# A hybrid decoder block on one core: the values' weights of one stage prepared earlier and partly on VectorE, and the last output weights prepared early

## The chip, the cores and the metric

The kernel runs on one core of a Trainium2 chip. The metric is device time in microseconds (us): the median of several executions. Before the change it is 588.81 us over 3 runs (588.73 to 589.13). The core has five engines that this document names as the profile does: PE (TensorE, the matrix engine; PEld is its weight load), DVE (VectorE), ACT (ScalarE), POOL (GpSimd) and SP (SyncE, which here issues all DMAs). Each engine serves its own queue of instructions in order and waits on semaphores for the others.

## The reference

One layer of a decoder block with two attention branches over 528 tokens (16 learned meta tokens and 512 real ones), width 1024:

```python
u = rmsnorm(h, pre_norm_g)
(cq, ckv, k_pe_raw, z_mla, fq, fk, fv, f_logit, z_fox, gate_a, gate_b) = split(u @ w_in)
# branch 1, MLA: 16 heads, low-rank queries, keys and values, rotary part of 32
q  = rmsnorm(cq)  @ w_uq
kv = rmsnorm(ckv) @ w_ukv
y_mla = (attention(q_m, k_m, v_mla) * silu(z_mla)) @ w_br_mla
# branch 2, FoX: 16 heads of 64, with a cumulative forget bias on the scores
cum = cumsum(log_sigmoid(f_logit + fox_forget_b))
y_fox = (attention(fq, fk, fv, bias=cum) * silu(z_fox)) @ w_br_fox
mixed = (sigmoid(gate_a) * y_mla + sigmoid(gate_b) * y_fox) @ w_out
out = h + rmsnorm(mixed, post_norm_g)          # meta tokens dropped
```

All inputs and outputs are float32. Attention is causal.

## The kernel before, in words

**Precision by halves.** Matmul operands are split into an upper half (`wh`, a rounded copy made on ACT) and a lower half (`wl`, the value less its upper half), and each product is three matmuls: upper by upper, upper by lower, lower by upper. `wsplit` (line 126) does this for a block of weights that was loaded as `wraw`: a cast 128x1024 on ACT (line 131), then a subtract on the engine that `low[0]` names, through `split_lo` (line 104). `low[0]` is POOL in the attention part, and DVE in the parts after it (line 1027). The tiles `wraw`, `wh` and `wl` come from a pool of three buffers each (line 84), so a cast waits for the buffer of an earlier block to be free.

**Units and fills.** A projection is a `unit` (line 176): a list of small steps of three matmuls each. Its `prep` splits the weights; its first step calls `prep` if nothing has called it before, and then issues the loads of the next three units. Steps of units are mixed between the attention's own work: `fills` has one list for each of 16 stages. A stage is one branch and one pair of heads, FoX and MLA in turn; stage 0 is FoX, stage 1 (`si == 1`) the MLA stage of the first pair. The fill of stage 1 is, in order: one transpose of values, the 8 steps of the FoX queries of the next pair (fq), the first 8 steps of its keys (fk), the 16 steps of its values (v, from step 17 on), and the last 8 steps of the keys.

**A stage** (lines 984 to 1016) takes scores on PE, evicts them with a mask or bias on DVE, takes exponentials on ACT (line 821), and normalises in two groups, `n0` (three query blocks) and `n1` (one): sums and reciprocals on DVE, then for each block and head a scaled upper half on ACT (line 850) and a lower half on DVE (line 851). POOL handles the leading 16 columns. The results are transposed by DMA for the value product (`ov`), which is written behind the scores of the next stage.

**What sets the order.** In the attention and after it, PE's matmuls run in the order in which the code writes them. The queues of the other engines are put in order when the program is built: each time an engine is free in the builder's own picture of the run, it takes the ready instruction with the smallest number, which is the place where it was written. `high_priority(offset=n)` writes instructions as if they stood n places earlier. `issue_after(x)` adds an edge: not ahead of x in x's queue. `keep_in_program_order` adds an edge to the instruction written just before on the same engine. In stage 1 the list `behind` holds the last exponential of the first three query blocks, so that the weight casts of this stage stand behind it on ACT (line 993). The order on the chip is then fixed.

In stage 1 before the change, v's weights are split when the fill comes to step 17, so in the code after both normalisations. SP issues v's load ahead of four small stores of rotary queries (`qpe_dram`) and of a transpose of values.

**The output projection** (from line 1262) is one level of Strassen's scheme: seven block products into accumulators X, Y, Z of two row blocks each, with sums of activations (`sh`, `sl`, `a1`, `a2`) and of weights (`tb`) made beforehand. `plain` and `summed` split the weights of half a product through the three-buffer pool. The last product adds the weight sum `tb[3]` times `a2` into X, which still holds the sum that rows 2 and 3 need in their other half; DVE must have read X before the last product writes on. Its weights `w4` are split in two pieces, the second behind the read of X. Then each row block is normalised: squares on ACT, `first_sum`, `scaled_g`, and `finish_t` (root, reciprocal, scale and residual) with two stores per block. Row blocks 0 and 1 are finished while the last products run, 2 and 3 at the end.

Of the kernel before, what the change touches and what calls it, by code (L numbers as in the profile page):

```python
# [17 lines left out]
ALU = mybir.AluOpType  # L18
# [4 lines left out]
D = 1024  # L23
# [5 lines left out]
EPS = 1e-6  # L29
# [26 lines left out]
def block_kernel(ctx: ExitStack, tc: tile.TileContext, x, meta_tokens, pre_norm_g, w_in, fox_forget_b,  # L56
                 mla_q_norm_g, mla_kv_norm_g, w_uq, w_ukv, w_br_mla, w_br_fox, w_out, post_norm_g,
                 rope_tok, rope_pe, out):
    nc = tc.nc
# [43 lines left out]
    def split_lo(eng, lo, src, hi):  # L103
        return eng.tensor_tensor(out=lo, in0=src, in1=f32(hi), op=ALU.subtract)  # L104
# [19 lines left out]
    low = [nc.gpsimd]  # L124
# [98 lines left out]
    def run(steps):  # L223
        for _, fn in steps:
            fn()
# [33 lines left out]
    with ExitStack() as ph:  # L259
# [33 lines left out]
        for c in range(4):  # L293
            r = pa.tile([128, 2, NSM], F32, tag="wsr", name=f"wsr{c}", bufs=4)
# [146 lines left out]
        pin = tc.keep_in_program_order  # L441
# [100 lines left out]
    with ExitStack() as att:  # L542
# [384 lines left out]
        for si, (br, pr) in enumerate(stages):  # L927
            last = si + 1 == len(stages)
            if not last:
                q, k, v = feed(*stages[si + 1])  # L930
            if br == 1:

                za, zb = z_unit(1, pr), z_unit(0, pr)
                fill = (vts[br, pr] if pr else begun) + za + q + zb[:3] + k + zb[3:5] + v + zb[5:]
            elif not last:

                fill = vts[br, pr] + q + k[:KD] + v + k[KD:]
            else:
                g = gate_unit()
                fill = vts[br, pr] + g + gate_unit() + gate_unit()  # L940
# [22 lines left out]
        for si, (br, pr) in enumerate(stages):  # L963
            last = si + 1 == len(stages)
            sc, n0, n1, va = attention(br, pr)

            fill = fills[si]
            sc()
            for fn in late:
                fn()  # L970
            if si == 0:

                run(fill[:5])
                run(vts[1, 0] + pe_rest)
                n0()
                bias(1)
                low[0] = nc.vector
                for ahead_ in [fn.prep for _, fn in fill[5:] if hasattr(fn, "prep")][:2]:
                    with tc.issue_after(whole[0]):
                        ahead_()  # L980
                low[0] = nc.gpsimd
                n1()
                run(fill[5:])
            else:
                if si == 1:
                    stores(2, 4)
                run(fill[:3])
                if si == 3:
                    stores(4, 8)
                run(fill[3:5])  # L990
                if si == 1:

                    behind[:] = exps[:1]
                if si == 2:
                    behind.clear()
                n0()
                if pr and not (br or last):
                    bias(pr + 1)
                run(fill[5:11])
                if br:  # L1000

                    behind[:] = [halved[("k", 1, pr), 1]]
                run(fill[11:12])
                if br:
                    behind.clear()
                n1()
                if not (br or last):
                    masked_bias()
                if 6 <= si < 8:

# [17 lines left out]
    with ExitStack() as mg:  # L1028
# [8 lines left out]
        tb = [m1.tile([128, HK, 512], F32, tag=f"tb{n}", name=f"tb{n}") for n in range(4)]  # L1037
        a1 = [m1.tile([128, HK, 256], F32R, tag=n, name=n) for n in ("a1h", "a1l")]
        a2 = [m1.tile([128, HK, S], F32R, tag=n, name=n) for n in ("a2h", "a2l")]
        mx = gT[0]  # L1040
        sh, sl = ([t.rearrange("p k s -> p (k s)")[:, 1024 * j : 1024 * j + 1024].rearrange("p (k s) -> p k s", k=HK)
                   for j in range(4)] for t in uT0)
# [164 lines left out]
        yo, xr = (o1.tile([128, 4, D], F32, tag=n, name=n) for n in ("yo", "xr"))  # L1207
        gp = o1.tile([128, D], F32, tag="gp", name="gp")
        ss = pad[:, 16:32].rearrange("p (t n) -> p t n", t=4)
# [10 lines left out]
        def summed(n, c):  # L1220
            uid[0] += 1
            raw = tb[n][:, 2 * c : 2 * c + 2].rearrange("p k f -> p (k f)")
            return by_k(wsplit((uid[0], raw, [(0, 1024)], 1024))[0], 2)

        def block(ps, a, t0, w, c, r, first, last, cs=slice(0, 512)):

            q = 0
            for kk in range(2):
                k = 2 * c + kk
                ts = slice(t0 + 128 * r, t0 + 128 * r + 128)  # L1230
                for x, b in ((a[0], w[0]), (a[1], w[0]), (a[0], w[1])):
                    mm(ps[r][:, cs], x[:, k, ts], b(kk)[:, cs], start=(first and c == 0 and q == 0), stop=(last and c == 1 and q == 5),
                       skip_group_check=True)
                    q += 1
# [7 lines left out]
        def squares_of(src, t, n, w=512):  # L1242
            nc.scalar.activation(jk[:, :w], src, AF.Square, accum_out=ss[:, t, n : n + 1])

        def first_sum(t, n):
            nc.vector.tensor_scalar(out=ss[:, t, 2:3], in0=ss[:, t, n : n + 1], scalar1=1.0 / D, scalar2=4.0 * EPS,
                                    op0=ALU.mult, op1=ALU.add)

        def scaled_g(t, sl, src=None):
            nc.vector.tensor_tensor(out=yo[:, t, sl], in0=yo[:, t, sl] if src is None else src, in1=gp[:, sl], op=ALU.mult)  # L1250

        def finish_t(t, n, order):
            nc.scalar.activation(ss[:, t, 3:4], ss[:, t, n : n + 1], AF.Sqrt, bias=ss[:, t, 2:3], scale=1.0 / D)
            nc.vector.reciprocal(ss[:, t, 3:4], ss[:, t, 3:4])
            for sl_ in order:
                nc.vector.scalar_tensor_tensor(out=yo[:, t, sl_], in0=yo[:, t, sl_], scalar=ss[:, t, 3:4],
                                               in1=xr[:, t, sl_], op0=ALU.mult, op1=ALU.add)
                nc.sync.dma_start(out2[128 * t : 128 * t + 128, sl_], yo[:, t, sl_])

        X, Z = ([op5.tile([128, 512], F32, tag="po", name=f"{n}{r}") for r in range(2)] for n in "xz")  # L1260
# [17 lines left out]
        product(Z, s_[3], 0, lambda c: plain(1, 1, c), False, True)  # L1278
        w7 = [summed(1, c) for c in range(2)]
        for r in range(2):  # L1280
            nc.vector.tensor_tensor(out=yo[:, r, N1], in0=Z[r], in1=yo[:, r, N1], op=ALU.add)
            squares_of(yo[:, r, N1], r, 1)
        w4 = [summed(3, 0)]
        for c in range(2):
            for r in range(2):
                block(X, s_[2], 0, w7[c], c, r, False, False)
                if c:
                    read = nc.vector.tensor_tensor(out=yo[:, 2 + r, N1], in0=X[r], in1=yo[:, 2 + r, N1], op=ALU.add)
                    if not r:
                        with tc.issue_after(read.ins):  # L1290
                            w4.append(summed(3, 1))
                    squares_of(yo[:, 2 + r, N1], 2 + r, 1)
                    first_sum(2 + r, 1)
        for r in range(2):
            scaled_g(r, N1)
            finish_t(r, 1, (N0, N1))
        for r in range(2):
            scaled_g(2 + r, N1)
        for r in range(2):
# [48 lines left out]
```

## Time and profile before

| | before |
|---|---|
| median of 3 runs | 588.81 us |
| the profiled execution | 589.07 us, span 587.1 us |
| granted PE clock, mean | 0.997 |
| PE busy | 577.8 us, 98% of the span |
| DVE busy | 419.4 us, 71% |
| ACT busy | 357.1 us, 61% |
| POOL busy | 199.0 us, 34% |
| DMA | 97.46 MB, mean 166 GB/s |

How to read the lines in the next part: a line of a timeline is the start in us from the begin of the span, the duration, the engine, the line of code, the operation, output and inputs by the program's names, the shape, and the count; in brackets the idle time of the engine before it and what ended it. In the list of waits the three numbers are us in total, times, and the longest. In the chain of waits a line is a start, a length, and what the chain was in. A table of stretches has, for each stretch, the busy time of PE, PEld, DVE, ACT and POOL with the number of instructions, then the granted PE clock, the share of the DMA engines and GB/s. A line of a DMA list ends with us from issue to landing. PE is busy nearly throughout, so what counts is where it stops.

### The profile page before, as it was taken

How to read it: one execution, taken by the hardware profiler on the slowest of the kernel's cores; microseconds unless marked ns; L12 is line 12 of the kernel's file. 1: busy time of each engine (PE TensorE's matmuls, PEld its weight loads, DVE VectorE, ACT ScalarE, POOL GpSimd, SP SyncE). 2: the span in 40 equal slices, each digit the busy share in tenths (PEclk: the TensorE clock that was granted, in tenths of full speed). 3: DMA queues.
4: the chain of work that ended last, by engine and by line, in shares of the span. 5: the costliest groups of instructions: out<-in, count | busy, mean ns of one | idle time of the engine just before them, and what ended most of it. 6: DMA issues, size and time to landing. Idle time of an engine off the chain costs nothing.

```text
span 587.1 us, 11116 instructions
## 1 busy us (share of the span) xinstructions
PE 577.8 (98%) x3841; PEld 497.7 (85%) x3841; DVE 419.4 (71%) x1155; ACT 357.1 (61%) x816; POOL 199.0 (34%) x271
## 2 busy tenths in 40 slices
PE   8999999999999999999999999999999999999996
PEld 6889888889889889888898898878998998888884
DVE  5854878884785775767758748896657876468957
ACT  7846774783783785767748747944343462443663
POOL 4317646464467472554544634510000000000000
PEclk9999999999999999999999999999999999999998
DMA  8535598999978999988987976877622544233603
GB/s 292 122 86 162 123 179 194 236 180 285 169 169 157 228 189 210 221 173 206 180 174 181 220 153 147 183 170 264 202 74 70 144 108 139 77 109 107 216 0 143
DMA packets 219999, 97.46 MB, mean 166 GB/s; under 512 B 131456, under 2 KB 209672, under 8 KB 219944
## 3 DMA queue, kind: packets, MB, share of 16 engines
q1 hardware_dynamic: 219944, 96.77, 69.5%
q8 instruction: 30, 0.49, 0.3%
q14 instruction: 25, 0.20, 0.1%
HBM read 62.36 MB, written 3.97 MB: 113 GB/s over the span
## 4 chain that ended last, share of the span: by engine, by line
PE 83%; POOL 1%; issue 0%; DVE 0%; DVEq 0%; ACT 0%; POOLq 0%
PE z L98 17%; PE pg L98 14%; PE v L98 8%; PE x L98 8%; PE py L98 7%; PE st L98 7%; PE fk L98 6%; PE fq L98 6%; PE ov L98 5%; PE y L98 2%; PE mq L98 2%; PE mk L98 1%; POOL wl L104 1%; PE ppe L98 0%; POOL mt L837 0%
## 5 line engine op out<-in xcount | busy, mean ns | idle before, releaser
L104 POOL TENSOR_TENSOR wl<-wraw,wh 128x1024 fp32r<-128x1024 f32 (+2 forms) x62 | 120.2, 1947 | 112.6 <-ACT wh L131 79.6
L131 ACT CAST wh<-wraw 128x1024 fp32r<-128x1024 f32 (+1 forms) x72 | 74.6, 1040 | 58.2 <-PE py L98 16.8
L821 ACT ACTIVATE sf<-sf,nb 128x272 f32<-128x272 f32 (+3 forms) x128 | 72.7, 569 | 11.2 <-DVE nb L786 10.2
L851 DVE SCALAR_TENSOR_TENSOR pn<-sf,ri,pn 128x512 f16<-128x512 f32 (+3 forms) x128 | 73.6, 641 | 2.1 <-ACT pn L850 1.9
L104 DVE TENSOR_TENSOR wl<-wraw,wh 128x512 fp32r<-128x512 f32 (+1 forms) x54 | 51.0, 947 | 28.6 <-ACT wh L1085 20.0
L850 ACT ACTIVATE pn<-sf,ri 128x128 f16<-128x128 f32 (+3 forms) x128 | 59.7, 548 | 0.0
L98 PE MATMUL z<-uTh,wh 128*128 128x512 f32 x128 | 50.9, 398 | 0.0
L98 PE MATMUL pg<-uTh,wh 128*128 128x512 f32 x128 | 50.2, 392 | 0.0
L98 PE MATMUL z<-uTl,wh 128*128 128x512 f32 x128 | 50.1, 391 | 0.0
L98 PE MATMUL z<-uTh,wl 128*128 128x512 f32 x128 | 50.0, 390 | 0.0
L98 PE MATMUL pg<-uTl,wh 128*128 128x512 f32 x128 | 49.9, 390 | 0.0
L98 PE MATMUL pg<-uTh,wl 128*128 128x512 f32 x128 | 49.8, 389 | 0.0
L98 PE MATMUL st<-hlk,hlq 64*128 64x272 f32 (+4 forms) x480 | 41.3, 299 | 0.0
L1085 ACT CAST wh<-wraw 128x512 fp32r<-128x512 f32 x28 | 17.3, 619 | 38.6 <-DVE wraw L1094 14.3
L701 DVE TENSOR_REDUCE vsc<-v 128x1 f32<-128x272 f32 (+1 forms) x32 | 13.2, 432 | 36.7 <-PE v L98 36.7
L98 PE MATMUL v<-uTh,wl 128*128 128x256 f32 (+1 forms) x128 | 36.6, 286 | 1.1 <-POOL wl L104 1.1
L98 PE MATMUL fk<-uTl,wh 128*128 128x256 f32 (+1 forms) x128 | 36.4, 285 | 0.0
L98 PEld LDWEIGHTS st<-hlk,hlq 64*128 64x128 f32 x480 | 33.0, 186 | 4.1 <-ACT vh L720 2.8
L98 PE MATMUL fk<-uTh,wh 128*128 128x256 f32 (+1 forms) x128 | 36.4, 285 | 0.0
L98 PE MATMUL v<-uTl,wh 128*128 128x256 f32 (+1 forms) x128 | 36.4, 285 | 0.0
L98 PE MATMUL fk<-uTh,wl 128*128 128x256 f32 (+1 forms) x128 | 36.4, 285 | 0.0
L98 PE MATMUL v<-uTh,wh 128*128 128x256 f32 (+1 forms) x128 | 36.4, 284 | 0.0
(285 smaller groups left out, 1611.5 us busy)
## 6 DMA issues: line engine op xcount, KB each, us to landing
wraw<-in_w_in_dram SPq DMA_DIRECT2D x56, 512.0 KB, 4.9
cbp<-c_dram SPq DMA_DIRECT2D x16, 264.0 KB, 3.9
wraw<-in_w_br_fox_dram SPq DMA_DIRECT2D x8, 512.0 KB, 4.7
tb<-in_w_out_dram SPq DMA_DIRECT2D x8, 512.0 KB, 5.2
wraw<-in_w_br_mla_dram SPq DMA_DIRECT2D x8, 512.0 KB, 4.1
wraw<-in_w_out_dram SPq DMA_DIRECT2D x6, 512.0 KB, 3.8
xr<-in_x_dram SPq DMA_DIRECT2D x4, 512.0 KB
out_dram<-yo SPq DMA_DIRECT2D x8, 256.0 KB, 2.0
```

Of the source, the lines that this page charges most:

```text
L98: nc.tensor.matmul(*a, **k)
L104: return eng.tensor_tensor(out=lo, in0=src, in1=f32(hi), op=ALU.subtract)
L131: nc.scalar.copy(wh[:, :n], raw[:, :n])
L701: nc.vector.tensor_reduce(out=sc[:, i : i + 1], in_=ps, op=ALU.max, axis=AX.X, apply_absolute_value=True)
L821: exps[b // 3] = nc.scalar.activation(sf, sf, AF.Exp, bias=sums["nb"][:, h, b : b + 1], scale=-1.0, accum_out=sums["su"][:, h, b : b + 1]).ins
L850: normed[:] = [nc.scalar.activation(hi, sf, AF.Copy, scale=rib).ins]
L851: nc.vector.scalar_tensor_tensor(out=lo, in0=sf, scalar=rib, in1=hi, op0=ALU.mult, op1=ALU.subtract)
L1085: nc.scalar.copy(to[0], src)
```

## The change

There are two edits.

In stage 1, after six further steps of the fill (which hold the split of fk's weights), the split of v's weights is written there and then, with a priority offset of 60, and its lower half goes to VectorE in place of GpSimd. It stands before the code of `n1`, and by its priority before `n0`. Step 17 later finds the weights split and only issues its matmuls and the next loads.

In the output projection the last product's weights no longer go through the three-buffer pool. A new function, `put_in`, splits both pieces into tiles whose last use lies several products back (`a1` and the first of the `sh`, `sl` pairs), and is written before the last two products. The vector instructions of the epilogue keep the order in which they are written (`pin`), and that order is changed: row blocks 0 and 1 are scaled and block 0 finished before the reads of X for rows 2 and 3, and block 1 is finished between these two reads.

```diff
@@ -997,6 +997,11 @@
                 if pr and not (br or last):
                     bias(pr + 1)
                 run(fill[5:11])
+                if si == 1:
+                    low[0] = nc.vector
+                    with tc.high_priority(offset=60):
+                        fill[17][1].prep()
+                    low[0] = nc.gpsimd
                 if br:
@@ -1222,6 +1227,15 @@
+        def put_in(n, c, to):
+            raw = tb[n][:, 2 * c : 2 * c + 2]
+            hi, lo = (t.rearrange("p k s -> p (k s)").rearrange("p (k f) -> p k f", k=2) for t in to)
+            nc.scalar.copy(hi, raw)
+            split_lo(nc.vector, lo, raw, hi)
+            return (lambda k: hi[:, k]), (lambda k: lo[:, k])
+
+        pin = tc.keep_in_program_order
...
         def first_sum(t, n):
-            nc.vector.tensor_scalar(...)
+            pin(nc.vector.tensor_scalar(...))
...
@@ -1278,22 +1292,22 @@
         w7 = [summed(1, c) for c in range(2)]
         for r in range(2):
-            nc.vector.tensor_tensor(out=yo[:, r, N1], in0=Z[r], in1=yo[:, r, N1], op=ALU.add)
+            pin(nc.vector.tensor_tensor(out=yo[:, r, N1], in0=Z[r], in1=yo[:, r, N1], op=ALU.add))
             squares_of(yo[:, r, N1], r, 1)
-        w4 = [summed(3, 0)]
+        w4 = [put_in(3, c, to) for c, to in enumerate((a1, s_[0]))]
+        for r in range(2):
+            scaled_g(r, N1)
+        finish_t(0, 1, (N0, N1))
         for c in range(2):
             for r in range(2):
                 block(X, s_[2], 0, w7[c], c, r, False, False)
-                if c:
-                    read = nc.vector.tensor_tensor(out=yo[:, 2 + r, N1], in0=X[r], in1=yo[:, 2 + r, N1], op=ALU.add)
-                    if not r:
-                        with tc.issue_after(read.ins):
-                            w4.append(summed(3, 1))
-                    squares_of(yo[:, 2 + r, N1], 2 + r, 1)
-                    first_sum(2 + r, 1)
         for r in range(2):
-            scaled_g(r, N1)
-            finish_t(r, 1, (N0, N1))
+            pin(nc.vector.tensor_tensor(out=yo[:, 2 + r, N1], in0=X[r], in1=yo[:, 2 + r, N1], op=ALU.add))
+            squares_of(yo[:, 2 + r, N1], 2 + r, 1)
+            if not r:
+                finish_t(1, 1, (N0, N1))
+        for r in range(2):
+            first_sum(2 + r, 1)
         for r in range(2):
             scaled_g(2 + r, N1)
```

The vector instructions in `scaled_g` and `finish_t` are pinned in the same way.

More of the change, by code (lines that the diff above doesn't have):

```diff
@@ L1245, in first_sum @@
         def first_sum(t, n):
-            nc.vector.tensor_scalar(out=ss[:, t, 2:3], in0=ss[:, t, n : n + 1], scalar1=1.0 / D, scalar2=4.0 * EPS,
-                                    op0=ALU.mult, op1=ALU.add)
+            pin(nc.vector.tensor_scalar(out=ss[:, t, 2:3], in0=ss[:, t, n : n + 1], scalar1=1.0 / D, scalar2=4.0 * EPS,
+                                        op0=ALU.mult, op1=ALU.add))
         def scaled_g(t, sl, src=None):
-            nc.vector.tensor_tensor(out=yo[:, t, sl], in0=yo[:, t, sl] if src is None else src, in1=gp[:, sl], op=ALU.mult)
+            pin(nc.vector.tensor_tensor(out=yo[:, t, sl], in0=yo[:, t, sl] if src is None else src, in1=gp[:, sl], op=ALU.mult))
         def finish_t(t, n, order):
             nc.scalar.activation(ss[:, t, 3:4], ss[:, t, n : n + 1], AF.Sqrt, bias=ss[:, t, 2:3], scale=1.0 / D)
-            nc.vector.reciprocal(ss[:, t, 3:4], ss[:, t, 3:4])
+            pin(nc.vector.reciprocal(ss[:, t, 3:4], ss[:, t, 3:4]))
             for sl_ in order:
-                nc.vector.scalar_tensor_tensor(out=yo[:, t, sl_], in0=yo[:, t, sl_], scalar=ss[:, t, 3:4],
-                                               in1=xr[:, t, sl_], op0=ALU.mult, op1=ALU.add)
+                pin(nc.vector.scalar_tensor_tensor(out=yo[:, t, sl_], in0=yo[:, t, sl_], scalar=ss[:, t, 3:4],
+                                                   in1=xr[:, t, sl_], op0=ALU.mult, op1=ALU.add))
                 nc.sync.dma_start(out2[128 * t : 128 * t + 128, sl_], yo[:, t, sl_])
```

## The prediction

> **What bounds the kernel now.** I read the page first, then the waits of the matmul engine, then the chain of waits, and only then the timelines around the two places that the change touches.
>
> ```profile
> span 587.1 us, 11116 instructions
> PE 83%; POOL 1%; issue 0%; DVE 0%; DVEq 0%; ACT 0%; POOLq 0%
> ```
>
> ```profile
> PE spun L98 <- DVE KPL L233: 1.5, 1, 1.5
> PE v L98 <- POOL wl L104: 1.1, 1, 1.1
> ```
>
> ```profile
> 91.04 2.52 POOL wl L104
> 93.56 0.04 issue
> 93.61 5.86 PE v L98 x46
> ...
> 575.53 5.75 PE x L98 x24
> ```
>
> PE is the bound. In the list of waits its largest stall outside the start is one of 1.1 us: the matmuls of v wait for a lower half (wl) made on POOL. From 93.61 to 581.29 the chain runs through PE alone. So a microsecond won or lost on PE at 93 us reaches the end in full: nothing later is idle and could absorb it. Behind 581.29 lies a tail of vector work and stores. The first edit aims at the 1.1 us stall, the second at the work around the tail.
>
> The stage around the stall, PE first, then POOL, ScalarE (ACT) and VectorE (DVE):
>
> ```profile
> 89.17 0.29 PE L98 MATMUL fk<-uTh,wh 128*128 128x272 f32 x1
> ...
> 89.42 0.29 PE L98 MATMUL fk<-uTh,wl 128*128 128x272 f32 x1
> ...
> 92.14 0.29 PE L98 MATMUL v<-uTh,wh 128*128 128x272 f32 x1
> 92.26 0.28 PE L98 MATMUL v<-uTl,wh 128*128 128x272 f32 x1
> 93.61 0.39 PE L98 MATMUL v<-uTh,wl 128*128 128x272 f32 x1 [1.06 <-POOL wl L104]
> ```
>
> ```profile
> 86.77 2.41 POOL L104 TENSOR_TENSOR wl<-wraw,wh 128x1024 fp32r<-128x1024 f32 x1
> ...
> 91.00 2.55 POOL L104 TENSOR_TENSOR wl<-wraw,wh 128x1024 fp32r<-128x1024 f32 x1
> ```
>
> ```profile
> 84.42 0.62 ACT L821 ACTIVATE sf<-sf,nb 128x400 f32<-128x400 f32 x1
> ...
> 85.03 1.04 ACT L131 CAST wh<-wraw 128x1024 fp32r<-128x1024 f32 x1
> 85.98 1.01 ACT L850 ACTIVATE pn<-sf,ri 128x512 f16<-128x512 f32 x2
> ```
>
> ```profile
> 89.61 1.04 ACT L131 CAST wh<-wraw 128x1024 fp32r<-128x1024 f32 x1
> ```
>
> Matched by order: the cast at 85.03 and the POOL subtract at 86.77 are fk's weights, ready at 89.18 for their first use at 89.42. The cast at 89.61 and the subtract at 91.00 are v's. Matmuls of this shape follow each other at 0.12 us (two steps from 89.17 to 89.42, one from 92.14 to 92.26), so v's third one was due at 92.38; it starts at 93.61, a loss of 1.23 us.
>
> **Edit 1, the halves of v.** It adds nothing and removes nothing. One ACT cast and one subtract are traced earlier, with a priority 60 instructions further up, and the subtract goes from POOL (2.55) to VectorE (1.22, first row below). No DMA is issued in it: v's load was issued by the unit before.
>
> ```profile
> L104 DVE TENSOR_TENSOR wl<-wraw,wh 128x1024 fp32r<-128x1024 f32 x26 | 31.7, 1222 | 8.5 <-ACT wh L131 8.1
> ```
>
> ```profile
> 86.73 3.00 DVE L851 SCALAR_TENSOR_TENSOR pn<-sf,ri,pn 128x512 f16<-128x512 f32 x1 [0.60 <-ACT pn L850]
> ```
>
> What it can win is the 1.23 us of v. On VectorE 1.22 us come in, and a blockage goes: the product at 86.73 takes 3.00 us while POOL's subtract of 86.77 runs. That is even or better, and beside PE's work.
>
> What it costs hangs on the place of the cast in ACT's queue, which is served in order, and on when v's raw weights are there:
>
> ```profile
> 78.47 0.56 SPq L92 DMA_DIRECT2D wraw<-in_w_in_dram  x1
> ```
>
> ```profile
> wraw<-in_w_in_dram SPq DMA_DIRECT2D x1, 512.0 KB, 10.7
> ```
>
> ```profile
> 86.00:89.00 3.00, 3.00 (x15) 2.49 (x14) 2.40 (x3) 3.00 (x8) 3.00 (x4) 1.00 0.15 43
> ```
>
> The load issued at 78.47 needs 10.7 us to land, so v's raw weights are complete only at about 89.2; from 86 to 89 the DMA moves 43 GB/s at a share of 0.15, with the stores to qpe_dram and a transpose issued behind this load. In the kernel before that is hidden: the cast stands behind all eight products (L850) and starts at 89.61. In the new one it may stand right behind the last exponential (84.42): its only order edge is to that instruction, and its priority lies ahead of fk's cast and of the products. The list order is made when the program is built, with its own picture of when a load lands, and that picture is early:
>
> ```profile
> 105.58 1.05 ACT L131 CAST wh<-wraw 128x1024 fp32r<-128x1024 f32 x1 [2.83 <-DMA wraw<-in_w_in_dram]
> ```
>
> Here ACT already stands 2.83 us before a cast whose load is not in, with exponentials queued behind it. I expect the same at 85.1 us, for longer.
>
> Step by step, if v's cast is first: ACT waits from 85.1 to 89.2, and v's cast runs. The next cast starts 0.95 later (85.03 to 85.98 is that spacing) at 90.15, and fk's upper half is there at 91.2. POOL's subtract follows at 91.25 and takes 2.41, to 93.65, and PE's third fk matmul starts 0.05 after that (as at 93.56 to 93.61, which I take for the hand-over before it too), at 93.7 instead of 89.42: **+4.3 us**. v's lower half is ready at 90.25 + 1.2 = 91.5, long before v starts at 96.4, so the old stall goes: **-1.2 us**. Queued behind the waiting cast are fk's cast, the eight products that fill ACT from 85.98 to 89.61, and the eviction of fq; the products start about 4 us late, and so do the transposes that the next ov needs.
>
> ```profile
> 98.35 3.23 SPq L92 DMA_TRANSPOSE pt<-pn  x1
> ```
>
> ```profile
> 104.45 0.62 PE L98 MATMUL ov<-pt,vp 80*64 80x512 f16 x4
> ```
>
> ```profile
> out_dram<-yo SPq DMA_DIRECT2D x8, 256.0 KB, 2.0
> ```
>
> The last of these is issued until 101.58; with the 2.0 us that the nearest listed small transfer needs to land it is in at about 103.6, 0.9 us ahead of ov. PE's own 3 us of delay move ov to 107.5, so this chain has 3 us more and I cost it at nothing. Without PE's delay it would be the next thing late: ov would be due at 104.45 - 1.2 = 103.2, and 0.4 us or more would come back.
>
> PE then has two pauses, 89.17 to 91.25 and 91.5 to 93.7, with two matmuls between. What the clock does in a pause can be read at the two ends of the run:
>
> ```profile
> 581.30:583.00 1.70, 0.00 (x0) 0.00 (x0) 1.59 (x4) 0.98 (x3) 0.00 (x0) 1.00 0.49 190
> 583.00:584.00 1.00, 0.00 (x0) 0.00 (x0) 1.00 (x2) 0.00 (x0) 0.00 (x0) 0.81 0.52 201
> 584.00:585.00 1.00, 0.00 (x0) 0.00 (x0) 0.24 (x1) 0.00 (x0) 0.00 (x0) 0.50 0.56 221
> ```
>
> ```profile
> 1.45 4.64 PE L98 MATMUL spun<-KPL 128*128 128x512 f32 x10 [1.45 <-DVE KPL L233]
> ```
>
> The granted clock goes from 1.00 to 0.50 within 583 to 584 (mean 0.81, so at about 583.6), 2.3 us after the last matmul. At the start ten matmuls of 512 columns take 4.64 us, 0.46 each, where in the last product they follow at 0.23 (574.90 and 575.13 below). So two pauses of 2.1 and 2.2 us in a stretch of 4.5 probably halve the clock, and getting it back costs 10 x 0.23 = **+2.3 us** (from 0, if it stays, to 2.9, if it takes a quarter longer). I take 2.3, the measured start.
>
> **Edit 2, the last weights.** Two casts (1.05 each) and two subtracts (1.22 each) move from around 570 to 576 into idle time before, into tiles that their last product has left; the DVE order is pinned. No load is added; the stores keep their number.
>
> ```profile
> 574.04 0.75 DVE L1256 SCALAR_TENSOR_TENSOR yo<-yo,pad,xr 128x512 f32<-128x512 f32 x1
> 574.70 0.69 DVE L1288 TENSOR_TENSOR yo<-x,yo 128x512 f32<-128x512 f32 x1
> ```
>
> ```profile
> 574.90 0.39 PE L98 MATMUL x<-wh,uTl 128*128 128x512 f32 x1
> 575.13 0.39 PE L98 MATMUL x<-wl,uTh 128*128 128x512 f32 x1
> 575.53 0.47 PE L98 MATMUL x<-wh,a2h 128*128 128x512 f32 x1
> ```
>
> The last product may overwrite X only when VectorE has read it (574.70 to 575.39); PE starts at 575.53 where 575.36 was due, and its next one 0.31 later instead of 0.23: 0.25 us lost. Without the subtract of the last weights VectorE is done with the first row block about a microsecond sooner and reads X when it is complete: **-0.2 us**. The other read of X now stands behind 1.4 us of finishing work, ends near 577.3, and is needed at 578.1.
>
> ```profile
> 560.09 1.23 DVE L104 TENSOR_TENSOR wl<-wraw,wh 128x1024 fp32r<-128x1024 f32 x1 [1.49 <-ACT wh L131]
> ```
>
> ```profile
> 581.31 0.58 ACT L1243 ACTIVATE jk<-x 128x512 f32<-128x512 f32 x1 [1.68 <-PE x L98]
> ```
>
> Gaps such as the 1.49 us before 560.09 hold a moved subtract; if one collides, a product waits a few tenths (the other end, +0.4). The tail does not shorten: it starts with the squares at 581.31, which wait for PE, and VectorE is free by then in both kernels.
>
> Sum against the profiled execution (589.07 us, span 587.1; 0.26 above the median of 588.81): +4.3 - 1.2 + 2.3 - 0.2 = +5.2, so 594.3 there and **594.0** against the median.
>
> **Rivals.** *The clock stays (591.7).* Neither pause alone is longer than the 2.3 us after which it fell at the end, and two matmuls lie between. Then the 2.3 falls away. For it: the 1.06 us pause at 93.61 left the clock alone; against it, 4.3 of 4.5 us idle. The Trainium skill's page "TensorE: Matmul & The Clock Gate", in Part 1, section "What's actually happening", gives the low clock after at least one idle window of about 3.4 us, free-running. By that rule this rival wins when no window lies in the pauses; the drop 2.3 us after the last matmul says that a window need not be idle throughout.
>
> *fk's cast goes first (587.6, the other side).* If the order puts fk's cast at 85.03 as now and v's next, fk is untouched and v's lower half is ready at 91.5 for 92.38: -1.2 and -0.2, with 0 to 0.4 back at ov because the products wait from 86 to 89.2. That is 587.4 to 587.8. It decides in which order two casts stand behind one exponential. Against it: v's priority is the higher, and its load was issued only 0.6 us after fk's.
>
> *No block (587.4).* If the order takes v's load as landed late, the cast falls among or behind the products: 588.81 - 1.2 - 0.2. For it speaks nothing in the trace; the 2.83 us wait speaks against it.
>
> *Worse.* If fk's cast also falls behind six of the eight products (6/8 of 3.63 us, 2.7), 597.
>
> **How the numbers follow.** Block with the clock halved 0.52, block with the clock kept 0.14, fk first 0.14, no block 0.15, worse or something else 0.05. The prediction is that of the likeliest, 594.0, its own range 592.8 to 595.2 (clock loss 1.7 to 2.9, edit 2 from -0.3 to +0.4). The range over the cases is 587.3 to 595.2. About 0.2%, 1.2 us, is what a measurement of this kernel can tell from no change. Slower: the first two and most of the rest, 0.70. The gains are -1.0 to -1.4 us, some inside that bound: faster 0.21, same 0.09.
>
> **What would show it.** Right: ACT idle for about 4 us behind the last exponential at 85.1, ended by a DMA; the two casts back to back from 89.2; PE waiting on fk's upper and lower halves in place of v's; granted clock at 0.50 for some 4 us from about 93; the products ending later; X read at 574.4 of the old clock with no gap in front of the last product. Wrong: fk's first matmul at 89.17 as before; no idle time of ACT at 85; or a load of v that lands well before 89.

## The result, and the profile after

The changed kernel takes 587.89 us (median) beside 588.88 us before. The ratio is 0.9983 with a 95% interval of 0.9975 to 0.9990: a gain of 0.17%, about 1 us. A second measurement beside other kernels gave 587.89 beside 589.01, a ratio of 0.9981 (0.9973 to 0.9990). The profiled execution took 587.82 us, and its page begins with

```profile
span 586.0 us, 11114 instructions
```

In the list of waits of the matmul engine (what it waited for: total, times, longest) the entry for v is gone, and a new one, for ov, stands in it (one of 0.6 us for psm, near the start of the program, is gone too, but comes back with 0.9 in a second profile of the same kernel):

```profile
PE spun L98 <- DVE KPL L233: 1.4, 1, 1.4
PE ov L98 <- DMA pt<-pn: 0.5, 2, 0.2
PE pt L101 <- DVE uTl L366: 0.3, 1, 0.3
```

The stage around the old stall, in the timeline after the change (start, duration, engine), ScalarE first, then GpSimd, VectorE, PE and the SP queue:

```profile
84.65 0.19 ACT L821 ACTIVATION_READ_ACCUMULATOR sf<-sf,nb 128x1 f32 x1
84.74 1.99 ACT L131 CAST wh<-wraw 128x1024 fp32r<-128x1024 f32 x2
86.63 3.74 ACT L850 ACTIVATE pn<-sf,ri 128x128 f16<-128x128 f32 x8
...
86.47 2.41 POOL L104 TENSOR_TENSOR wl<-wraw,wh 128x1024 fp32r<-128x1024 f32 x1
...
86.76 3.19 DVE L104 TENSOR_TENSOR wl<-wraw,wh 128x1024 fp32r<-128x1024 f32 x1 [0.93 <-ACT wh L131]
89.88 4.05 DVE L851 SCALAR_TENSOR_TENSOR pn<-sf,ri,pn 128x128 f16<-128x128 f32 x8
...
92.23 0.28 PE L98 MATMUL v<-uTl,wh 128*128 128x272 f32 x1
92.36 0.29 PE L98 MATMUL v<-uTh,wl 128*128 128x272 f32 x1
...
90.46 0.42 SPq L92 DMA_DIRECT2D wraw<-in_w_in_dram  x1
91.30 3.98 SPq L92 DMA_TRANSPOSE pt<-pn  x2
```

Two casts run back to back at 84.74, with no wait between the last exponential and them, and the eight products follow. GpSimd's subtract (fk's lower half) starts at 86.47, about where it did before (86.77), and VectorE's (v's) at 86.76, as the second cast ends. So the first of the two casts is fk's and the second is v's. v's lower half is there at 89.95, and its third matmul starts at 92.36, 0.13 behind its neighbour at 92.23: the stall of 1.23 us is gone. On the SP queue a load of raw weights now stands ahead of the four transposes; before, all four stood ahead of it:

```profile
91.07 10.51 SPq L92 DMA_TRANSPOSE pt<-pn  x4
101.67 2.29 SPq L92 DMA_DIRECT2D wraw<-in_w_in_dram  x3
```

What lets it go earlier is v's raw buffer, whose last reader is v's subtract (in a second profile, below, the load is issued at 90.65 and the subtract ends at 90.63). The chain of waits shows where it ends:

```profile
98.61 4.67 DMA pt<-pn
103.28 0.14 issue
103.41 2.04 PE ov L98 x26
```

The last transpose, issued at 98.61, lands at 103.28, and ov waits for it. The second edit shows in the timeline of the last product (X read on VectorE, then PE):

```profile
573.20 0.69 DVE L1305 TENSOR_TENSOR yo<-x,yo 128x512 f32<-128x512 f32 x1 [0.17 <-PE x L98]
...
574.13 0.39 PE L98 MATMUL x<-wl,uTh 128*128 128x512 f32 x1
574.36 0.39 PE L98 MATMUL x<-a1h,a2h 128*128 128x512 f32 x1
```

The read of X starts 1.16 us before the last product (574.36) needs its place and ends 0.47 us before it, and the matmuls go on at 0.23.

A ledger from the starts of PE's matmuls is the best way to compare these profiles, because the first fk matmul already differs by up to 0.96 us between kernels that are alike up to there (88.85 to 89.81). All points are starts of matmuls, and each stretch begins where the one on its left ends: the first of fk and of v in this stage, the first of the ov that follows, the last of the program. The kernels further down the table are described in the next part:

| profile | fk first to v first | v first to ov first | ov first to last matmul | last matmul to end |
|---|---|---|---|---|
| before | 2.96 | 12.32 | 476.42 | 6.23 |
| after | 2.96 | 11.30 | 476.26 | 6.29 |
| after, second profile | 2.96 | 11.41 | 476.24 | 6.31 |
| edit 1 alone | 2.96 | 12.84 | 478.12 | 6.51 |
| edit 2 alone | 2.96 | 12.32 | 476.21 | 6.23 |
| v's cast first | 7.67 | 11.12 | 476.20 | 6.29 |
| load put back | 2.96 | 10.99 | 476.19 | 6.32 |
| load put back, second profile | 2.96 | 10.99 | 476.18 | 6.29 |
| lower half on GpSimd | 2.96 | 11.97 | 476.18 | 6.23 |
| engine only | 2.96 | 12.95 | 476.20 | 6.30 |
| both halves on VectorE, load put back | 2.96 | 10.99 | 476.20 | 7.41 |
| v's cast behind seven products | 2.96 | 10.99 | 476.20 | 6.52 |
| stores later | 2.96 | 10.99 | 483.59 | 6.29 |
| v's cast first, stores later | 6.92 | 11.37 | 476.20 | 6.29 |

From before to after: -1.02 between v and ov, -0.16 behind it, +0.06 in the tail, -0.02 up to fk: -1.14, which is the difference of the spans. Free of waits the second stretch takes 10.99, so the old stall was worth 1.33 and 0.31 of it came back at ov.

### The profile page after: what moved, and what is told of

It reads as the page before. It is cut to its first block, busy times and chain, and to the rows that moved or that the text cites. A ratio compares the mean times of both kernels' runs of the same rounds, so it can differ in the third digit from the quotient of the medians.

```text
span 586.0 us, 11114 instructions
## 1 busy us (share of the span) xinstructions
PE 577.9 (99%) x3841; PEld 498.4 (85%) x3841; DVE 416.3 (71%) x1156; ACT 357.9 (61%) x816; POOL 197.2 (34%) x270
## 4 chain that ended last, share of the span: by engine, by line
PE 91%; DMA 3%; DVE 3%; issue 1%; SPq 0%; ACT 0%; POOL 0%; DVEq 0%; POOLq 0%
PE z L98 17%; PE pg L98 15%; PE v L98 9%; PE fq L98 8%; PE x L98 8%; PE fk L98 8%; PE py L98 7%; PE st L98 7%; PE ov L98 5%; PE y L98 2%; DMA pt<-pn 2%; PE mq L98 2%; PE psm L98 2%; PE ppe L98 1%; DVE uTl L366 1%
## 5 line engine op out<-in xcount | busy, mean ns | idle before, releaser
L104 POOL TENSOR_TENSOR wl<-wraw,wh 128x1024 fp32r<-128x1024 f32 (+2 forms) x61 | 117.9, 1940 | 112.2 <-ACT wh L131 80.5
L104 DVE TENSOR_TENSOR wl<-wraw,wh 128x512 fp32r<-128x512 f32 (+1 forms) x55 | 54.2, 987 | 27.7 <-ACT wh L1090 19.7
L851 DVE SCALAR_TENSOR_TENSOR pn<-sf,ri,pn 128x512 f16<-128x512 f32 (+3 forms) x128 | 66.9, 588 | 1.7 <-ACT pn L850 1.7
```

What stands on the lines that cost most here:

```text
L851: nc.vector.scalar_tensor_tensor(out=lo, in0=sf, scalar=rib, in1=hi, op0=ALU.mult, op1=ALU.subtract)
```

## The experiments

Three questions: is the predicted mechanism (v's cast first, ScalarE blocked) real where the order is so; what is the new wait at ov; and which part of the change does what.

**Each edit alone.** Edit 1 on the kernel before:

```diff
                 run(fill[5:11])
+                if si == 1:
+                    low[0] = nc.vector
+                    with tc.high_priority(offset=60):
+                        fill[17][1].prep()
+                    low[0] = nc.gpsimd
```

> Edit 1 alone, on the kernel before. Theory A (fk's cast is first on ScalarE, v's second, so fk is untouched): the stall of 1.1 to 1.2 us at v's third matmul goes, a wait of 0.2 to 0.4 us at the next ov comes, and the time is about 0.9 us below the kernel before (588.0 beside 588.9). Theory B (edit 1 is worth nothing in the end, because the time comes back at ov or later, and edit 2 carries the gain): within 0.3 us of the kernel before. By the recorded main case (v's cast waits in front of fk's) it would be 4 to 6 us above.

Measured: 588.66 us beside 588.91, ratio 0.9995 (0.9985 to 1.0006), single times from 588.02 to 591.81. The profiled execution was the longest of them. Its chain of waits, and its windows from 104 us (PE busy, PEld, DVE, ACT, POOL, granted clock, DMA share, GB/s):

```profile
100.47 4.67 DMA pt<-pn
105.14 0.14 issue
105.28 3.71 PE ov L98 x26
```

```profile
104.00:106.00 2.00, 0.72 (x5) 0.43 (x7) 2.00 (x17) 1.80 (x7) 1.12 (x1) 0.85 0.99 227
106.00:108.00 2.00, 2.00 (x14) 1.38 (x12) 1.38 (x9) 2.00 (x7) 0.00 (x0) 0.50 1.09 315
108.00:110.00 2.00, 2.00 (x18) 1.68 (x15) 0.94 (x4) 0.60 (x3) 0.00 (x1) 0.79 1.23 280
```

The stall at v is gone here too, but the last transpose was issued 1.9 us later than in the profile after, ov waited 1.78 us, and the clock fell to 0.50 behind it: 1.85 us between v and ov over the clean 10.99, and 1.7 us more behind ov than before. So the new wait at ov isn't a fixed 0.2 us; in a bad execution it costs more than edit 1 gains. Theory A's 588.0 was reached only by the shortest times. Why the median stands 0.8 us above the changed kernel's, where edit 2 is worth 0.2, isn't settled; in this profile the tail is longer by 0.2 us.

Edit 2 alone is the changed kernel without those five lines.

> Edit 2 alone, on the kernel before. Theory A: the late read of X in front of the last product goes, 0.2 to 0.25 us of PE time, 588.65 beside 588.9; the stall at v's third matmul stays at 1.1 us. Theory B (edit 2 carries the gain): 587.9. If a subtract moved into an earlier gap delays a product, 588.9 to 589.3.

Measured: 588.92 beside 588.91, ratio 0.9999 (0.9990 to 1.0007). The timeline shows what was expected, the old stall (first row) and no gap ahead of the last product (at 576.00):

```profile
94.25 0.39 PE L98 MATMUL v<-uTh,wl 128*128 128x272 f32 x1 [1.06 <-POOL wl L104]
...
575.77 0.39 PE L98 MATMUL x<-wl,uTh 128*128 128x512 f32 x1
576.00 0.39 PE L98 MATMUL x<-a1h,a2h 128*128 128x512 f32 x1
```

The stretch behind ov is 476.21, 0.21 below before. That is the size expected, and too small for the times, whose interval is 1 us wide. Theory B falls: edit 2 doesn't carry the gain. The medians of the two edits alone, 0.25 us faster and no change, don't add up to the 1 us of both together; with intervals about 1 us wide the times don't settle that. What divides the gain is the ledger of the profiles: 1.0 us between v and ov, 0.2 behind it.

**v's cast first.** The two casts exchanged, so that the queue is the one the prediction had assumed (fk's cast ordered behind v's); this also puts the load back behind the transposes:

```diff
+                if si == 1:
+                    ...
+                        fill[17][1].prep()
+                    ...
+                    behind[:] = cast[:]
                 run(fill[5:11])
```

> The changed kernel with fk's and v's casts exchanged on ScalarE, so that v's stands first behind the last exponential, as the prediction had assumed. Theory A (the prediction's mechanism, with v's load landing at 89 as in the profile before): ScalarE waits about 4 us ended by the load, fk's third matmul starts near 93.7 in place of 89.4, 592 to 594 us. Theory B (the load usually lands near 84.2, as in the profile after, and the landing at 89.1 was one execution's): no wait on ScalarE; fk's lower half, made on GpSimd from a cast 1 us later, is late by about 0.4 us, so 588.1 to 588.4.

Measured: 593.41 us beside 588.91, ratio 1.0074 (1.0062 to 1.0086). ScalarE, GpSimd and PE, and then the clock:

```profile
89.25 1.99 ACT L132 CAST wh<-wraw 128x1024 fp32r<-128x1024 f32 x2 [3.83 <-DMA wraw<-in_w_in_dram]
...
91.32 2.44 POOL L104 TENSOR_TENSOR wl<-wraw,wh 128x1024 fp32r<-128x1024 f32 x1 [3.04 <-ACT wh L132]
...
91.30 0.39 PE L98 MATMUL fk<-uTh,wh 128*128 128x272 f32 x1 [1.68 <-ACT wh L132]
...
93.82 0.59 PE L98 MATMUL fk<-uTh,wl 128*128 128x272 f32 x1 [2.01 <-POOL wl L104]
```

```profile
92.00:94.00 2.00, 0.18 (x1) 0.18 (x2) 2.00 (x2) 2.00 (x5) 1.77 (x1) 0.60 0.58 166
94.00:96.00 2.00, 2.00 (x9) 2.00 (x10) 2.00 (x6) 1.34 (x3) 0.00 (x0) 0.50 0.28 59
...
98.00:100.00 2.00, 2.00 (x14) 2.00 (x13) 0.37 (x1) 0.79 (x2) 0.00 (x0) 0.69 1.13 211
```

Every step of the prediction's main case is here: the wait of 3.8 us ended by the load, the two pauses of PE, the halved clock. Theory A holds, and theory B's 588.1 to 588.4 didn't occur in any of five times.

**Where the load lands.** The changed kernel again, unaltered:

> The changed kernel unaltered, as the neighbour of the next three and for a second look at when v's load lands. Theory A (the landing differs from execution to execution, near 84.4 or near 89, and the changed kernel pays for the late one): median near 587.9, single times between 587.2 and 589.2; if this profile shows the load landing near 89, ScalarE waits about 2.5 us in front of v's cast and PE waits 1.5 us or more at the next ov; if near 84.4, no wait on ScalarE and about 0.2 us at ov. Theory B (the landing is fixed by the order of the queue): 84.2 again.

Measured: 587.89 us, single times from 587.22 to 588.89. In this profile ScalarE did wait for the load, behind fk's cast:

```profile
88.22 1.05 ACT L131 CAST wh<-wraw 128x1024 fp32r<-128x1024 f32 x1 [2.40 <-DMA wraw<-in_w_in_dram]
...
89.31 1.32 DVE L104 TENSOR_TENSOR wl<-wraw,wh 128x1024 fp32r<-128x1024 f32 x1 [3.43 <-ACT wh L131]
90.55 3.90 DVE L851 SCALAR_TENSOR_TENSOR pn<-sf,ri,pn 128x128 f16<-128x128 f32 x8
...
103.29 2.04 PE L98 MATMUL ov<-pt,vp 80*64 80x512 f16 x26 [0.35 <-DMA pt<-pn]
...
90.65 0.37 SPq L92 DMA_DIRECT2D wraw<-in_w_in_dram  x1
```

The list of transfers gives v's load (512 KB, us from issue to landing) as 5.5 in the first profile of this kernel and 9.8 in the second:

```profile
wraw<-in_w_in_dram SPq DMA_DIRECT2D x1, 512.0 KB, 5.5
```

```profile
wraw<-in_w_in_dram SPq DMA_DIRECT2D x1, 512.0 KB, 9.8
```

So the landing differs from execution to execution, and theory A holds in that. Its other half doesn't: the wait of 2.4 us cost ov 0.35 us, not 1.5. VectorE, which spent 3.19 us on v's subtract while GpSimd's was running, needs 1.32 when it comes later, so the products end at 94.45 in place of 93.93.

To see whether the four stores to qpe_dram behind the load make it late, they were moved to the end of the stage:

```diff
                 if si == 1:
-                    stores(2, 4)
                 run(fill[:3])
...
                 run(fill[12:])
+                if si == 1:
+                    stores(2, 4)
```

> The changed kernel with the four stores to qpe_dram, which stand right behind v's load on the SP queue, moved to the end of this stage. Theory A (these stores share a DMA engine with one sixteenth of v's load and now and then hold it up until they are through, at 89): with them gone the load lands below 85, ScalarE never waits for it, and the time is 587.2 to 587.6 with a narrow spread. Theory B (the late landing has another cause): the load still lands near 89 in some executions, and the time stays near 587.9. If reading the stored rows back becomes late for the next q, 1 us or more is added in either case.

Measured: 594.35 us, ratio 1.0080 (1.0064 to 1.0096). The clause on the stored rows being late is what happened: they are read back at 109.03, the transposes of the next stage stand behind that on the queue, and its ov waits 4.86 us.

```profile
109.03 0.34 SPq L92 DMA_DIRECT2D QP<-qpe_dram  x1
...
127.49 3.84 PE L98 MATMUL ov<-pt,vp 80*64 80x512 f16 x26 [4.86 <-DMA pt<-pn]
```

The time says nothing on the question then; the landing does, together with the next kernel, which has the exchanged casts and the stores later (both edits above):

> The casts of fk and v exchanged as in the kernel with v's cast first (593.4), and the stores to qpe_dram moved to the end of the stage. Theory A (the 4 us block is the late landing, and that comes from the stores): no wait on ScalarE behind the last exponential, fk's lower half late by about 0.4 us, 587.8 to 588.3. Theory B (the block comes from v's cast being first, whatever the stores do): 592.5 to 594.5 again.

Measured: 591.61 us, ratio 1.0039 (1.0027 to 1.0051), between the two theories and in neither.

```profile
85.24 1.99 ACT L132 CAST wh<-wraw 128x1024 fp32r<-128x1024 f32 x2
...
89.58 2.66 POOL L104 TENSOR_TENSOR wl<-wraw,wh 128x1024 fp32r<-128x1024 f32 x1
...
92.29 0.39 PE L98 MATMUL fk<-uTh,wl 128*128 128x272 f32 x1 [2.51 <-POOL wl L104]
```

ScalarE doesn't wait: with the load landing early, the block of 4 us is gone though v's cast is first. The 2.5 us of waiting that remain are GpSimd's, which in this order does the small products of its own ahead of fk's subtract. Counted from the first fq matmul, fk's third is 2.7 us later here than in the kernel with the load put back, for 4.1 with v's cast first and the load late; and the granted clock went to 0.50 here too (the window from 94 to 96 has 0.50). So the wait for the load is only a part of what v's cast costs when it stands first. The landings, from the trace's records of the sixteen completions that each transfer has (us; the fifteenth and last of v's load, and the last of the stores):

| profile | load issued | fifteenth part | last part | last store |
|---|---|---|---|---|
| before | 78.47 | 83.52 | 89.13 | 89.25 |
| after, second | 78.42 | 83.05 | 88.20 | 88.23 |
| v's cast first | 79.00 | 84.12 | 89.23 | 89.29 |
| load put back, second | 79.15 | 83.99 | 89.13 | 89.15 |
| after | 78.70 | 83.71 | 84.18 | 88.88 |
| load put back | 78.78 | 83.66 | 84.44 | 88.83 |
| stores later | 78.67 | 84.20 | 84.21 | 108.88 |
| v's cast first, stores later | 78.88 | 84.58 | 84.58 | 106.99 |

With the stores behind it, the load was late in 7 of the 12 profiles, and then its last sixteenth came with the last store. Without them it was early in 2 of 2. That fits the stores holding up one sixteenth; but 5 of the 12 were early with the stores in place, so two early ones can be chance, and what decides in which execution it happens stays open.

**The new wait at ov.** The load of raw weights that had moved ahead of the transposes, put back behind the last of them:

```diff
+                        turned_last[:] = [dma(ptt[:, 0 : 2 * n, 128 * b : 128 * b + 128], ...)]
...
-                run(fill[12:])
+                with tc.issue_after(turned_last[0]) if si == 1 else nullcontext():
+                    run(fill[12:])
```

> The changed kernel with one load of raw weights (the one that the earlier release of v's buffer let pass ahead of the four pt transposes) put back behind the last transpose on the SP queue. Theory A (this load delays the transposes and makes the new wait of 0.2 us at ov): the last transpose lands 0.2 us or more sooner, the wait at ov goes, and the time is 0.2 to 0.4 us below the changed kernel (587.6). Theory B (ov is late because PE comes to it 1.2 us earlier and the products have not become as much faster): the wait and the time stay (587.9). If the load itself then becomes late for its cast near 101, slower by some tenths.

Measured: 587.58 us beside 588.91, ratio 0.9978 (0.9969 to 0.9987). One of its twelve executions took 957.41 us, at a mean granted clock of 0.558, which nothing here explains; the ratio leaves it out, and without it the median is 587.44. The chain of waits goes through PE alone:

```profile
101.04 2.19 PE st L98 x30
103.23 1.97 PE ov L98 x26
```

The same kernel a second time:

> The changed kernel with the load put back behind the last transpose, a second time beside other neighbours. Theory A (the load ahead of the transposes costs the changed kernel 0.3 to 0.4 us): 587.5 to 587.7 and no wait at ov in the profile, also if v's load lands near 89. Theory B (the first result was chance): 587.9, or a wait at ov.

Measured: 587.76 beside 589.10, ratio 0.9977 (0.9969 to 0.9986). This profile had the late landing (2.44 us of wait on ScalarE), and ov still didn't wait. In both the stretch from v to ov is 10.99. So the load ahead of the transposes makes the wait, 0.3 to 0.4 us of it in the profiles after; the medians agree in direction, 0.1 to 0.3 us, though their intervals overlap with the changed kernel's. No kernel here was faster.

**Place or engine.** The early place kept, the lower half left on GpSimd:

```diff
                 if si == 1:
-                    low[0] = nc.vector
                     with tc.high_priority(offset=60):
                         fill[17][1].prep()
-                    low[0] = nc.gpsimd
```

> The changed kernel with the early place of v's cast kept, but the lower half left on GpSimd. Theory A (the early cast alone removes the stall): GpSimd starts v's subtract right behind fk's at about 88.9 and ends near 91.4, a microsecond ahead of its use at 92.4, so v does not wait; the products on VectorE are held up by two subtracts of GpSimd instead of one and end near 96, so ov waits 0.3 to 0.8 us; 587.9 to 588.3. When v's load lands near 89, GpSimd ends at 92.5 and v waits one or two tenths. Theory B (VectorE is what does it): v still waits about a microsecond, 588.7.

Measured: 588.50 beside 589.10, ratio 0.9992 (0.9983 to 1.0001).

```profile
90.47 8.03 DVE L851 SCALAR_TENSOR_TENSOR pn<-sf,ri,pn 128x128 f16<-128x128 f32 x8 [4.02 <-ACT pn L850]
...
103.07 0.96 PE L98 MATMUL st<-hlk,hlq 64*128 64x288 f32 x8 [0.17 <-DVE hlk L104]
104.42 2.04 PE L98 MATMUL ov<-pt,vp 80*64 80x512 f16 x26 [0.39 <-DMA pt<-pn]
```

v doesn't wait, as theory A has it. But the eight products take 8.03 us with GpSimd's subtract among them and 3.90 without it (second profile after; the load was late in both), so st and ov start late: 0.98 of the 1.33 us come back between v and ov. The early place removes the stall; that VectorE does the subtract keeps the gain. With the place alone the time isn't clear of no change.

The other way round, the old place on ScalarE and only the engine changed:

```diff
                 n1()
+                if si == 1:
+                    low[0] = nc.vector
+                    fill[17][1].prep()
+                    low[0] = nc.gpsimd
```

> The changed kernel with v's cast left in its old place on ScalarE, behind the eight products, and only the engine of the lower half changed to VectorE. Theory A (the place is what does it): the subtract stands behind all products on VectorE, which end near 93.2, so the lower half is there at about 94.4 for 92.4: v waits 1.5 to 2.1 us, more than before, and the time is 588.8 to 589.5. Theory B (the faster engine alone removes the stall): no wait at v, 587.6.

Measured: 589.53 beside 589.10, ratio 1.0007 (0.9998 to 1.0016).

```profile
93.48 1.22 DVE L104 TENSOR_TENSOR wl<-wraw,wh 128x1024 fp32r<-128x1024 f32 x1
...
94.75 0.39 PE L98 MATMUL v<-uTh,wl 128*128 128x272 f32 x1 [1.69 <-DVE wl L104]
```

The subtract stands behind all products on VectorE, and v waits longer than before. So the engine alone gains nothing: the place removes the stall, and both together give the gain.

**Two further versions.** With the load put back, fk's lower half on VectorE as well:

> The changed kernel with the load kept behind the last transpose, and fk's lower half on VectorE as well, so that no subtract of GpSimd falls between the products. Theory A (behind the last expected wait only PE is left): v's subtract takes 1.2 us instead of 3.2, the products end 1 to 2 us earlier, PE waits for nothing here, and the time is that of the kernel with only the load put back, 587.4 to 587.8. Theory B (the two engines' holding each other up still costs time): 0.2 us or more below it.

Measured: 588.65 beside 589.10, ratio 0.9992 (0.9983 to 1.0000), 0.9 us slower than with the load put back alone, though PE waits for nothing and all stretches up to the last matmul are the same. The ledger has it in the tail: 7.41 in place of 6.32. The transfers from 582.7 us in this kernel:

```profile
q14 instruction: 1, 0.01, 0.6%
out_dram<-yo SPq DMA_DIRECT2D x1, 256.0 KB, 3.2
```

The last store of the program needs 3.2 us to land where it needed 2.0 with only the load put back, and a packet of instructions is moved in the same stretch, which isn't the case there before the store has landed. All eleven times are above 588.3, so it wasn't one execution alone that was slower. Whether the move of fk's subtract to VectorE brings that packet isn't shown: the next kernel makes the same move, and its last store needs 2.0 us.

The last kernel makes both lower halves on VectorE, has the load behind the transposes, and puts v's cast behind seven of the eight products:

```diff
                             nc.vector.scalar_tensor_tensor(out=lo, in0=sf, scalar=rib, in1=hi, op0=ALU.mult,
                                                            op1=ALU.subtract)
+                            done_ += 1
+                            if hook and g and done_ == 1:
+                                low[0] = nc.vector
+                                hook.pop()()
+                                low[0] = nc.gpsimd
```

> The changed kernel, but v's cast stands on ScalarE behind seven of the eight products (it starts at about 89.1) instead of ahead of them, both lower halves (fk's and v's) are made on VectorE, and the load of raw weights stays behind the last transpose. Theory A (what hurts the changed kernel is that the products queue behind a cast that may wait for its load): no wait at v's third matmul (lower half ready at about 92.2 for 92.4), none at ov, wherever the load lands; 587.0 to 587.4 and a spread of half a microsecond. Theory B (the spread has another cause): median near 587.6 to 587.9 with single times up to 589. If the subtract comes too late on VectorE, a few tenths at v.

Measured: 588.08 beside 589.01, ratio 0.9983 (0.9974 to 0.9991), single times from 587.41 to 588.67. In the profile PE waits neither at v nor at ov, as expected, but the spread is 1.26 us, beside 1.67 for the changed kernel in the same round: theory A's half microsecond and its 587.0 to 587.4 fall, and the median is above theory B's 587.6 to 587.9 too. The profiles' starts alone (fk's first matmul, 88.85 to 89.81) spread over 1 us, and this stage has no part in that.

## Why the prediction was wrong

*The step that failed* is "v's cast is first". The prediction took the priority, 60 instructions further up, to decide between the casts of fk and v, and so made a block in front of fk's weights the likeliest case. The order built has fk's cast first and v's second; fk starts at 89.15 (89.17 before), so the +4.3 us at fk and the +2.3 us of the clock never arose. Why the builder put v's cast second isn't shown by any run; that v's weights weren't ready in its picture by then would be one reason, that 60 places don't make v's number the smaller one another. The rival "fk's cast goes first" is what happened. It gave 587.4 to 587.8, and 587.89 was measured.

*The mechanism behind that step was right where its condition is met.* With v's cast put first, 593.41 us were measured for 594.0 predicted. Counted from the first fq matmul, and compared with the kernel with the load put back, fk's third matmul (93.82) is 4.1 us late for the 4.3 of the sum; all stretches up to ov together are 6.7 us longer, which leaves 2.6 for the clock where 2.3 had been taken. The two waits, 1.68 and 2.01, are the two pauses predicted. But the prediction put all of the 4.3 down to the load: with the load early, 2.7 us of the delay were still there, by way of GpSimd. And the lower end of its range doesn't follow from its terms: 594.0 less 0.6 for the clock and 0.1 for edit 2 is 593.3, where it has 592.8.

*The landing at 89.2* had been taken from one profile as fixed. It is one of two cases, near 84.4 and near 89, and the profile after shows the other.

*"No DMA is issued in it"* was true and missed the point: an earlier last use of a buffer releases the load that waits for it, and that load went past four transposes on SP. The rival had allowed 0 to 0.4 us at ov, for another reason (products waiting for v's load); the 0.31 and 0.42 us measured come from the load, since they vanish when it is put back, late landing or not. That the allowance holds them, or nearly, is luck.

*The subtract on VectorE* was put at 1.22 and took 3.19 beside GpSimd's subtract in the profile after. It is still in time, by 2.4 us, so the sum didn't change.

*Edit 2* was right in place and size: X is read when it is complete, the gap of 0.25 us in front of the last product is gone, and the stretch behind ov is 0.16 to 0.24 us shorter for the 0.2 predicted. No moved subtract collided, and the tail stayed as it was.

## What to carry to other kernels

When a change moves a waiting instruction in an in-order queue, find out which of its neighbours really stands in front of it before pricing the block: here the order of two casts decided between a loss of 4.5 us and a gain of 1 us. Follow every buffer whose last use moves to the load that waits for it, and that load to what it now passes on its queue. A landing read from one profile is one draw; where a sum hangs on it, look at how far the other parts of the same transfer, or other transfers of its size, were ahead of it.

## What was unexpected of the hardware

A load of 512 KB landed 5.5 us after its issue in one execution and 9.8 us after it in the next, of the same program; in the late case fifteen sixteenths were in at 83.05 and the last at 88.20, 0.03 us ahead of the last of four stores issued behind it.

The pause that halves the clock can be shorter than the 2.3 us the prediction read from the end of the run: 1.78 us in front of ov did it in edit 1 alone, while 1.69 us in front of v did not in the kernel with only the engine changed:

```profile
94.00:96.00 2.00, 1.25 (x10) 1.25 (x11) 1.64 (x3) 0.18 (x1) 1.75 (x1) 1.00 1.02 192
```

The low stretch, worked out from the mean clocks of the windows shown (0.85 over 2 us is 0.6 us at 0.50, and so on), lasted 0.6 + 2.0 + 0.84 = 3.4 us in edit 1 alone and 1.6 + 2 + 2 + 1.24 = 6.8 us with v's cast first, where the window from 96 to 98 is at 0.50 as well. One and two times 3.4: that agrees with the free-running window of about 3.4 us which the Trainium skill's page "TensorE: Matmul & The Clock Gate" gives in Part 1, "What's actually happening". The pauses in front of these two drops were shorter than a window, so a whole idle window isn't needed here.

The records of the granted clock in the traces say it more closely: the stretches at full clock are whole multiples of 3.413 us (29 times up to the drop in edit 1 alone, 25 times with v's cast first, 169 or 170 times where nothing drops before the end). Laid out in such steps, the 1.78 us of edit 1 lie inside one step, and the 1.69 us are cut by a boundary into 1.08 and 0.61. What counts seems to be the idle time within a step: it was 1.78, 2.01 and 2.27 us ahead of the drops in edit 1 alone, in v's cast first with the stores later, and in v's cast first. The limit isn't sharp by this count, since in the second profile after, 1.86 us of idle within one step at the end of the program did not lower the clock.

VectorE's subtract took 3.19 us where it ran beside GpSimd's from 86.76, and 1.32 in the second profile, where it came after GpSimd's; there a small cast of GpSimd that began after it, at 89.49, took 1.26 us, for 0.33 in the profile before. The Trainium skill's page "SBUF — State Buffer" says in "Who interferes with whom" that the two engines share a port pair under an exclusive lock; the trace agrees, the subtract ending about 1.1 us after GpSimd's had ended at 88.88.
